# The y products of two state-space head pairs in one step, and the p·v products of two attention pairs in one step

## The chip, the cores and the metric

The kernel runs on one core of a Trainium2 chip. The metric is the device time of one execution in microseconds (us). Three executions of the kernel before took 1226.97, 1227.45 and 1230.41 us; the median is 1227.45 us.

A core has a matrix engine (TensorE, PE in the rows; its weight loads stand apart as PEld), a vector engine (VectorE, DVE), an activation engine (ScalarE, ACT), a general engine (GpSimd, POOL) and a queue that issues transfers (SyncE, SP). TensorE writes its products to banks of PSUM, from which VectorE or ScalarE take them.

## The reference, cut to what matters

Two layers on 256 tokens of width 1024. Each layer has a mixer, with sparse attention (16 heads of 64) and a state-space part (4 groups of 8 heads of 64) in parallel, and then a feed-forward part. The two products that the change touches are the last line of attention and the diagonal term of the scan:

```python
p = jax.nn.softmax(s, axis=-1).astype(v.dtype)
return jnp.einsum("bhqk,bqkhd->bqhd", p, vg)
...
cb = jnp.einsum("bclgn,bcsgn->bgcls", cm_c, bm_c)
y_diag = jnp.einsum("bgcls,bgrcls,bcsgrp->bclgrp", cb, decay, xs_c)
```

All is in float32. The sequence is a single chunk of 256 tokens, so that `y_diag` is the whole scan. In each layer this makes 8 pairs of attention heads and 16 pairs of state-space heads.

## The kernel before, in words

**The stream.** Most of TensorE's work is the big projections. A weight unit of 512 columns by 4 blocks of 128 rows lands in `st`, ScalarE rounds it into `wh`, and VectorE makes the rest `wl = st - wh` ("the split"). The activations are kept as two such parts as well (`h` for the normed input, `u` for attention's output). Each product is three matmuls in rounded float32: high by high, high by low, low by high. A unit's matmuls run feature block by feature block; after each 12 of them a function `pump` is called.

**The side work.** Attention, the scan and the norms are generators, kept in lists (`hot`, `warm`, `calm`, `cool`). Every `pump` may advance each list by one step. A step first yields a `Need`: it goes on when the tiles that it names are expected to be ready and the number of PSUM banks that it names is free. Only the first generator of `calm` advances, and `attention` and `ssd` are both in `calm`, one behind the other. A planner with its own table of costs estimates when each instruction ends; from that it decides when a step is due, and in what order VectorE, ScalarE and GpSimd get their work. So the order of the instructions is fixed when the program is built, and a change to one step can move many others. `cool` holds the stream of modulation weights (`ad`), which VectorE sums into `adacc` (eight steps, then a small product with `ones`).

**`ssd(g)`** runs for each group of four head pairs. It transposes the inputs into two tiles `xdt`, and then loops over n. A step with n below 4 makes the decay tile `e` of pair n (a product with `sel`, three activations, and a multiplication with `cbm` on VectorE). Two steps later come the y products of that pair: into one bank `py`, four matmuls, two of 256 and two of 128 columns, whose weights are 64 columns wide, so that the two heads of the pair stand in the two halves of the bank. VectorE adds the result to `x_[i]` with the weight `dsk`. When all four are done `ssd_norm(g)` starts; in it `spread` sends the reciprocal root over the partitions, and the normed results are split in two parts for the product with `w_ssm_o`. The last two of group 3 lie in the two `xdt` tiles.

**`attention`** runs twice for each layer, with four pairs. A step makes the scores of pair n, two steps later the transposes of its weights into `pT`, and one step after that its p·v products, four matmuls of the same shapes as those of y, into a bank `po`; `hi_lo` takes that bank in two parts.

In the rows, both `e` and `pT` bear the name `p`; `bk` is a PSUM bank, and `bk<-p,xdt` is a y product, `bk<-p,u` a p·v product. "128*64" is the shape of the weights: 128 rows by 64 columns. A float32 matmul that isn't rounded shows as two matmuls in the trace, so a y block of four shows as x8. All operations bear the line of the helper that records them (L209).

Of the kernel before, what the change touches and what calls it, by code (L numbers as in the profile page):

```python
# [15 lines left out]
ALU = mybir.AluOpType  # L16
# [3 lines left out]
P = 128  # L20
S = 256
# [25 lines left out]
def trunk(ctx, tc, x, c, positions, w_ada, b_ada, norm1_g, w_in, q_norm_g, k_norm_g, ssm_conv_w, ssm_conv_b,  # L47
# [1289 lines left out]
    def mixer(l, link, link_out):  # L1337
# [244 lines left out]
        def attention(heads):  # L1582
# [4 lines left out]
            for n in range(len(pairs) + TD + PD):  # L1587
                if n < len(pairs):
                    i = pairs[n]
                    yield Need(qT[i], kT[i], m01, banks=2)  # L1590
                    pss = [bank(), bank()]
                    both(pss, qT[i], kT[i], False)
                    done(qT[i], kT[i])
                    for j in range(2):
                        mm(pss[j][:, 0:384], nident, m01, False, True)
                    pe = pes[n] = hold(w_tile("pe", [P, 2, 384]))
                    mx = w_tile("mx", [P, 2, 2])
                    sums = w_tile("sums", [P, 2, 2])
                    with urgent():
                        for j in range(2):  # L1600
                            V.tensor_reduce(mx[:, j, 0:1], pss[j][:, 0:P], axis=AX.X, op=ALU.max)
                            V.tensor_reduce(mx[:, j, 1:2], pss[j][:, P:384], axis=AX.X, op=ALU.max)
                            V.tensor_tensor(mx[:, j], mx[:, j], nrq[:, 2 * i + j, :], op=ALU.mult)
                        for j in range(2):
                            for t, cs in HALF:
                                A.activation(pe[:, j, cs], pss[j][:, cs], AF.Exp, scale=rq[:, 2 * i + j, t:t + 1],
                                             bias=mx[:, j, t:t + 1], accum_out=sums[:, j, t:t + 1])
                    yield Need(sums, on="dve")
                    with urgent():
                        V.reciprocal(sums, sums)  # L1610
                        for j in range(2):
                            for t, cs in HALF:
                                G.tensor_scalar(pe[:, j, cs], pe[:, j, cs], sums[:, j, t:t + 1], 0.0, op0=ALU.mult, op1=ALU.add)
                if n - TD in pes:
                    pe = pes.pop(n - TD)
                    yield Need(pe, banks=2)
                    pT = pTs[n - TD] = hold(w_tile("pT", [P, 2, 384]))
                    pts = [bank(), bank()]
                    for j in range(2):
                        for b in range(3):  # L1620
                            T.transpose(pts[j][:, b * P:b * P + P], pe[:, j, b * P:b * P + P], ident)
                    done(pe)
                    with urgent():
                        for j in range(2):
                            A.activation(pT[:, j], pts[j][:, 0:384], AF.Copy)
                if n - TD - PD in pTs:
                    pT = pTs.pop(n - TD - PD)
                    i = pairs[n - TD - PD]
                    yield Need(pT, *vt[0][i // 4], *vt[1][i // 4], banks=1)
                    po = bank()  # L1630
                    for t, cs, src in ((0, slice(0, S), slice(0, S)), (1, slice(P, S), slice(S, 384))):
                        for j in range(2):
                            hh = 2 * i + j
                            vs = slice((hh % 4) * 64, (hh % 4) * 64 + 64)
                            mm(po[64 * j:64 * j + 64, cs], vt[t][hh // 8][(hh % 8) // 4][:, vs], pT[:, j, src], t == 0, t == 1)
                    done(pT)
                    if i % 2 == 1:
                        done(*(vt[t][i // 4][(i % 4) // 2] for t in range(2)))
                    with urgent():
                        hi_lo(po[:, 0:S], oT, i)  # L1640


        def ev_conv(base, dst, then=None):
# [44 lines left out]
        def ssd(g):  # L1688
# [12 lines left out]
            for n in range(4 + 2):  # L1701
                if n < 4:
# [13 lines left out]
                    yield Need(e, on="dve")  # L1716
                    with urgent():
                        V.tensor_tensor(e, e, cbm[g][:, None, :].to_broadcast([P, 2, 384]), op=ALU.mult)
                if n >= 2:
                    i = n - 2  # L1720
                    e = es.pop(i)
                    yield Need(e, cbm[g], *xdt, banks=1)
                    py = bank()
                    for cs, x, src in ((slice(0, S), xdt[0], slice(0, S)), (slice(P, S), xdt[1], slice(S, 384))):
                        for j in range(2):
                            hs = slice((2 * i + j) * 64, (2 * i + j) * 64 + 64)
                            mm(py[64 * j:64 * j + 64, cs], x[:, hs], e[:, j, src], x is xdt[0], x is xdt[1])
                    done(e)
                    m = 4 * g + i
                    with urgent():  # L1730
                        V.scalar_tensor_tensor(x_[i], x_[i], dsk[:, l, m:m + 1], py[:, 0:S], op0=ALU.mult, op1=ALU.add)
            while None in z_:
                yield
            warm.append(ssd_norm(g))
# [203 lines left out]
```

## Time and profile before

| | |
|---|---|
| median of three executions | 1227.45 us |
| the profiled execution, its own time | 1227.39 us |
| its span in the trace | 1225.7 us |
| TensorE busy | 1201.3 us, 98% of the span |
| VectorE busy | 991.4 us, 81% |
| ScalarE busy | 775.3 us, 63% |
| GpSimd busy | 494.1 us, 40% |

The span is the time from the first to the last instruction; 1.7 us of the execution lie outside it. "Busy" of TensorE counts a matmul from its start to its modelled end, and matmuls overlap, so the distance from one start to a later one tells more than the durations. In a window's row the fields are the stretch, its length, busy time (with the number of instructions) of TensorE, its weight loads, VectorE, ScalarE and GpSimd, then the granted TensorE clock (1.00 is 2.4 GHz, 0.50 is 1.2 GHz), the share of the DMA engines and GB/s.

### The profile page before, as it was taken

The page shows a single profiled execution, that of the slowest core. Times are in us where ns is not written, and L with a number is a line of the kernel's source. Part 1 is how long each engine was busy: PE and PEld are TensorE (multiplying, and loading weights), DVE is VectorE, ACT ScalarE, POOL GpSimd, SP SyncE. Part 2 cuts the span into 40 slices and gives each one's busy share as a digit, 9 for nine tenths or more (in the row PEclk, how much of TensorE's full clock was granted, in tenths as well). Part 3 has the DMA queues.
Part 4 walks back from the last instruction along what each step waited for, and adds up shares of the span by engine and source line. Part 5 has one row for each costly group of instructions (what it writes and reads, how often), then busy time and mean ns, then how long its engine had stood idle before and what let it go on. Part 6 is the DMA issues. An engine that isn't in the chain of part 4 may idle for free.

```text
span 1225.7 us, 24837 instructions
## 1 busy us (share of the span) xinstructions
PE 1201.3 (98%) x9835; PEld 1118.9 (91%) x9835; DVE 991.4 (81%) x1549; ACT 775.3 (63%) x1397; POOL 494.1 (40%) x503
## 2 busy tenths in 40 slices
PE   8999999999999999999999999999999999999998
PEld 7777898899988999999998778899999999999998
DVE  5488998778988789989767899888778757988863
ACT  4365577767865468778535557878578535877742
POOL 2163442216445225766202356314605313457710
PEclk9999999999999999999999999999999999999999
DMA  9765656655557666777665566264664665667551
GB/s 307 241 208 178 200 180 212 207 193 195 190 181 241 232 198 198 240 240 260 206 229 186 204 206 199 87 215 134 216 218 156 211 220 189 190 198 232 179 205 64
DMA packets 158665, 246.55 MB, mean 201 GB/s; under 512 B 11868, under 2 KB 66870, under 8 KB 158549
## 3 DMA queue, kind: packets, MB, share of 16 engines
q1 hardware_dynamic: 157989, 244.77, 60.1%
q8 instruction: 77, 1.26, 0.4%
q14 instruction: 39, 0.32, 0.1%
q0 software_dynamic: 288, 0.19, 0.1%
q10 hardware_dynamic: 272, 0.00, 0.0%
HBM read 243.89 MB, written 1.05 MB: 200 GB/s over the span
## 4 chain that ended last, share of the span: by engine, by line
PE 81%; DVE 12%; ACT 2%; issue 2%; POOL 1%; DMA 1%; SPq 0%; DVEq 0%; POOLq 0%; ACTq 0%
PE bk L209 81%; DVE wl L209 5%; DVE w L209 2%; DVE adacc L209 1%; ACT wh L209 1%; DVE p L209 1%; DVE u L209 1%; DVE t L209 1%; ACT w L209 1%; POOL rr L209 0%; DMA ad<-in_w_ada_dram 0%; POOL rows L209 0%; DVE top L209 0%; DVE mx L209 0%; POOL w L209 0%
## 5 line engine op out<-in xcount | busy, mean ns | idle before, releaser
L209 PE MATMUL bk<-h,wh 128*128 128x256 f32 x3296 | 588.1, 281 | 1.2 <-ACT h L209 1.1
L209 PEld LDWEIGHTS bk<-h,wh 128*128 128x128 f32 x3296 | 500.9, 189 | 12.0 <-issue 8.2
L209 DVE TENSOR_TENSOR wl<-st,wh 128x2048 fp32r<-128x2048 f32 (+1 forms) x200 | 439.8, 2206 | 67.3 <-ACT wh L209 67.0
L209 PE MATMUL bk<-h,wl 128*128 128x256 f32 x1648 | 457.9, 278 | 1.7 <-DVE wl L209 1.7
L209 ACT ACTIVATE wh<-st 128x2048 fp32r<-128x2048 f32 (+1 forms) x200 | 352.8, 1770 | 154.8 <-PE bk L209 129.9
L209 POOL TENSOR_TENSOR w<-w,w 128x254 f32<-128x254 f32 (+2 forms) x213 | 254.9, 1209 | 252.7 <-DVE w L209 173.4
L209 PEld LDWEIGHTS bk<-h,wl 128*128 128x128 f32 x1648 | 309.9, 188 | 2.4 <-DVE wl L209 1.9
L209 PE MATMUL bk<-u,wh 128*128 128x256 f32 x1312 | 232.6, 280 | 0.0
L209 PEld LDWEIGHTS bk<-u,wh 128*128 128x128 f32 x1312 | 199.3, 189 | 2.4 <-issue 2.4
L209 PE MATMUL bk<-u,wl 128*128 128x256 f32 x656 | 182.7, 278 | 0.6 <-DVE wl L209 0.6
L209 PE MATMUL bk<-wh,h 128*128 128x512 f32 x448 | 145.9, 402 | 3.1 <-DVE t L209 2.0
L209 ACT ACTIVATE w<-bk,vec 128x256 f32<-128x256 f32 (+2 forms) x256 | 119.7, 519 | 37.5 <-DVE w L209 26.0
L209 PEld LDWEIGHTS bk<-u,wl 128*128 128x128 f32 x656 | 123.2, 188 | 0.8 <-DVE wl L209 0.8
L209 DVE SCALAR_TENSOR_TENSOR adacc<-ad,chalf,adacc 128x512 f32<-128x512 f32 x140 | 119.0, 850 | 0.5
L209 PEld LDWEIGHTS bk<-wh,h 128*128 128x128 f32 x448 | 81.5, 188 | 23.9 <-issue 3.7
L209 POOL TENSOR_TENSOR u<-u,u 128x256 f32<-128x256 f32 (+1 forms) x56 | 74.1, 1348 | 63.1 <-DVE u L209 37.3
L209 PE MATMUL bk<-wl,h 128*128 128x512 f32 x224 | 88.7, 396 | 2.8 <-DVE wl L209 2.7
L209 DVE SCALAR_TENSOR_TENSOR w<-bk,vec,w 128x255 f32<-128x255 f32 (+1 forms) x176 | 80.3, 476 | 13.4 <-ACT w L209 11.9
L209 POOL TENSOR_TENSOR rr<-ss,mhalf 128x16 f32<-128x16 f32 x8 | 35.6, 4454 | 77.7 <-DVE ss L209 77.7
L209 POOL TENSOR_SCALAR p<-p,sums 128x128 f32<-128x128 f32 x64 | 35.6, 574 | 55.5 <-DVE sums L209 47.8
L209 ACT ACTIVATE u<-bk 128x128 f32<-128x128 f32 (+2 forms) x128 | 32.1, 321 | 39.8 <-PE bk L209 39.2
L209 PEld LDWEIGHTS bk<-wl,h 128*128 128x128 f32 x224 | 42.1, 188 | 13.4 <-DVE wl L209 4.6
(225 smaller groups left out, 1399.6 us busy)
## 6 DMA issues: line engine op xcount, KB each, us to landing
st<-in_w_in_dram SPq DMA_DIRECT2D x80, 1024.0 KB, 5.1
st<-in_w_up_dram SPq DMA_DIRECT2D x88, 512.0 KB, 5.2
ad<-in_w_ada_dram SPq DMA_DIRECT2D x160, 256.0 KB, 5.4
st<-in_w_down_dram SPq DMA_DIRECT2D x20, 1024.0 KB, 5.0
st<-in_w_ssm_o_dram SPq DMA_DIRECT2D x16, 1024.0 KB, 5.0
st<-in_w_ada_dram SPq DMA_DIRECT2D x16, 512.0 KB, 9.6
st<-in_w_attn_o_dram SPq DMA_DIRECT2D x8, 1024.0 KB, 5.1
st<-in_w_out_dram SPq DMA_DIRECT2D x8, 1024.0 KB, 5.1
```

The source lines that it names most:

```text
L209: w.issue()
```

## The change

Both loops now wait until two pairs are ready and write their products one behind the other. In `ssd` the y products of pairs 0 and 1 stand in step 3 (before: 2 and 3), those of pairs 2 and 3 in step 5 (before: 4 and 5). In `attention` the p·v products of pairs 0 and 1 stand in step 4 (before: 3 and 4), ahead of that step's transposes (before: behind them), and those of pairs 2 and 3 in step 6 (before: 5 and 6). The `Need` names both pairs' tiles, and two banks in place of one. Matmuls and their operands stay the same.

```diff
--- before.py
+++ after.py
@@ -1611,6 +1611,21 @@
                         for j in range(2):
                             for t, cs in HALF:
                                 G.tensor_scalar(pe[:, j, cs], pe[:, j, cs], sums[:, j, t:t + 1], 0.0, op0=ALU.mult, op1=ALU.add)
+                if (n - TD - PD) % 2 == 1 and n - TD - PD in pTs:
+                    two = [(pTs.pop(k), pairs[k]) for k in (n - TD - PD - 1, n - TD - PD)]
+                    yield Need(*(t for pT, i in two for t in (pT, *vt[0][i // 4], *vt[1][i // 4])), banks=2)
+                    for pT, i in two:
+                        po = bank()
+                        for t, cs, src in ((0, slice(0, S), slice(0, S)), (1, slice(P, S), slice(S, 384))):
+                            for j in range(2):
+                                hh = 2 * i + j
+                                vs = slice((hh % 4) * 64, (hh % 4) * 64 + 64)
+                                mm(po[64 * j:64 * j + 64, cs], vt[t][hh // 8][(hh % 8) // 4][:, vs], pT[:, j, src], t == 0, t == 1)
+                        done(pT)
+                        if i % 2 == 1:
+                            done(*(vt[t][i // 4][(i % 4) // 2] for t in range(2)))
+                        with urgent():
+                            hi_lo(po[:, 0:S], oT, i)
                 if n - TD in pes:
                     pe = pes.pop(n - TD)
                     yield Need(pe, banks=2)
@@ -1623,21 +1638,6 @@
                     with urgent():
                         for j in range(2):
                             A.activation(pT[:, j], pts[j][:, 0:384], AF.Copy)
-                if n - TD - PD in pTs:
-                    pT = pTs.pop(n - TD - PD)
-                    i = pairs[n - TD - PD]
-                    yield Need(pT, *vt[0][i // 4], *vt[1][i // 4], banks=1)
-                    po = bank()
-                    for t, cs, src in ((0, slice(0, S), slice(0, S)), (1, slice(P, S), slice(S, 384))):
-                        for j in range(2):
-                            hh = 2 * i + j
-                            vs = slice((hh % 4) * 64, (hh % 4) * 64 + 64)
-                            mm(po[64 * j:64 * j + 64, cs], vt[t][hh // 8][(hh % 8) // 4][:, vs], pT[:, j, src], t == 0, t == 1)
-                    done(pT)
-                    if i % 2 == 1:
-                        done(*(vt[t][i // 4][(i % 4) // 2] for t in range(2)))
-                    with urgent():
-                        hi_lo(po[:, 0:S], oT, i)
 
 
         def ev_conv(base, dst, then=None):
@@ -1716,19 +1716,19 @@
                     yield Need(e, on="dve")
                     with urgent():
                         V.tensor_tensor(e, e, cbm[g][:, None, :].to_broadcast([P, 2, 384]), op=ALU.mult)
-                if n >= 2:
-                    i = n - 2
-                    e = es.pop(i)
-                    yield Need(e, cbm[g], *xdt, banks=1)
-                    py = bank()
-                    for cs, x, src in ((slice(0, S), xdt[0], slice(0, S)), (slice(P, S), xdt[1], slice(S, 384))):
-                        for j in range(2):
-                            hs = slice((2 * i + j) * 64, (2 * i + j) * 64 + 64)
-                            mm(py[64 * j:64 * j + 64, cs], x[:, hs], e[:, j, src], x is xdt[0], x is xdt[1])
-                    done(e)
-                    m = 4 * g + i
-                    with urgent():
-                        V.scalar_tensor_tensor(x_[i], x_[i], dsk[:, l, m:m + 1], py[:, 0:S], op0=ALU.mult, op1=ALU.add)
+                if n in (3, 5):
+                    two = [(i, es.pop(i)) for i in (n - 3, n - 2)]
+                    yield Need(*(e for _, e in two), cbm[g], *xdt, banks=2)
+                    for i, e in two:
+                        py = bank()
+                        for cs, x, src in ((slice(0, S), xdt[0], slice(0, S)), (slice(P, S), xdt[1], slice(S, 384))):
+                            for j in range(2):
+                                hs = slice((2 * i + j) * 64, (2 * i + j) * 64 + 64)
+                                mm(py[64 * j:64 * j + 64, cs], x[:, hs], e[:, j, src], x is xdt[0], x is xdt[1])
+                        done(e)
+                        m = 4 * g + i
+                        with urgent():
+                            V.scalar_tensor_tensor(x_[i], x_[i], dsk[:, l, m:m + 1], py[:, 0:S], op0=ALU.mult, op1=ALU.add)
             while None in z_:
                 yield
             warm.append(ssd_norm(g))
```

In the order on TensorE, the first y products of layer 0 (group 0) stood like this before, between two matmuls of the stream; those of the next pair came 40 rows later, between two others:

```order
L209 MATMUL bk_3179<-u_2536,wh_3011 128x256
L209 MATMUL bk_3179<-u_2535,wl_3012 128x256
L209 MATMUL bk_3239<-p_495_3118,xdt_488_3062 64x256 x2
L209 MATMUL bk_3239<-p_495_3118,xdt_489_3063 64x128 x2
L209 MATMUL bk_3179<-u_2362,wh_3011 128x256
L209 MATMUL bk_3179<-u_2363,wh_3011 128x256
```

and now:

```order
L209 MATMUL bk_3175<-u_3027,wh_3096 128x256
L209 MATMUL bk_3175<-u_3026,wl_3097 128x256
L209 MATMUL bk_3276<-p_495_3116,xdt_488_3060 64x256 x2
L209 MATMUL bk_3276<-p_495_3116,xdt_489_3061 64x128 x2
L209 MATMUL bk_3277<-p_498_3155,xdt_488_3060 64x256 x2
L209 MATMUL bk_3277<-p_498_3155,xdt_489_3061 64x128 x2
L209 MATMUL bk_3175<-u_2899,wh_3096 128x256
L209 MATMUL bk_3175<-u_2900,wh_3096 128x256
```

The two blocks of four matmuls have become neighbours. The same is so at all 16 pairs of y blocks in the two layers.

The first p·v products of layer 0's attention stood alone as well, as this piece of the difference shows:

```order
 L209 MATMUL bk_2287<-h_473,wh_2103 128x256
 L209 MATMUL bk_2287<-h_472,wl_2104 128x256
-L209 MATMUL bk_2361<-p_329_2062,u_1084 64x256 x2
-L209 MATMUL bk_2361<-p_329_2062,u_1086 64x128 x2
 L209 MATMUL bk_2287<-h_297,wh_2103 128x256
 L209 MATMUL bk_2287<-h_298,wh_2103 128x256
```

They stand one step later now, with those of the second pair behind them and the transposes of `p_286` moved on:

```order
 L209 MATMUL bk_2287<-h_473,wh_2103 128x256
 L209 MATMUL bk_2287<-h_472,wl_2104 128x256
-L209 MATMUL bk_2394<-ident,p_286_1757 128x128 x3
-L209 MATMUL bk_2395<-ident,p_286_1757 128x128 x3
+L209 MATMUL bk_2376<-p_329_2062,u_1084 64x256 x2
+L209 MATMUL bk_2376<-p_329_2062,u_1086 64x128 x2
+L209 MATMUL bk_2379<-p_371_2333,u_1084 64x256 x2
+L209 MATMUL bk_2379<-p_371_2333,u_1086 64x128 x2
 L209 MATMUL bk_2286<-h_594,wh_2202 128x256
 L209 MATMUL bk_2286<-h_595,wh_2202 128x256
```

All eight pairs of p·v blocks are joined in this way. In all, 48 blocks have become 24.

On VectorE, the rows ahead of one split in layer 0 (the second unit that is split after the multiplications of group 2 have begun) were these before:

```order
L209 SCALAR_TENSOR_TENSOR w_636_4105<-bk_3925,vec_293,w_636_4105 128x255
L209 SCALAR_TENSOR_TENSOR w_636_4105<-bk_3925,vec_293,w_636_4105 128x254
L209 SCALAR_TENSOR_TENSOR adacc_3854<-ad_4001,chalf,adacc_3854 128x512
L209 TENSOR_TENSOR p_650_4197<-p_650_4197,cbm_348_2159 128x768
L209 SCALAR_TENSOR_TENSOR u_4060<-w_628_4059,w_626_4057 128x256
L209 SCALAR_TENSOR_TENSOR w_640_4109<-bk_3925,vec_293,w_640_4109 128x255
L209 SCALAR_TENSOR_TENSOR w_640_4109<-bk_3925,vec_293,w_640_4109 128x254
L209 SCALAR_TENSOR_TENSOR adacc_3854<-ad_4052,chalf,adacc_3854 128x512
L209 SCALAR_TENSOR_TENSOR u_3673<-u_3673,dsk,bk_4284 128x256
L209 SCALAR_TENSOR_TENSOR u_4108<-w_638_4107,w_636_4105 128x256
L209 SCALAR_TENSOR_TENSOR u_4112<-w_642_4111,w_640_4109 128x256
L209 TENSOR_TENSOR wl_4134<-st_3831,wh_4133 128x2048
```

and are these now:

```order
L209 SCALAR_TENSOR_TENSOR u_4067<-w_628_4066,w_626_4064 128x256
L209 SCALAR_TENSOR_TENSOR u_3699<-u_3699,dsk,bk_4209 128x256
L209 SCALAR_TENSOR_TENSOR u_4071<-w_632_4070,w_630_4068 128x256
L209 SCALAR_TENSOR_TENSOR w_640_4113<-bk_3938,vec_293,w_640_4113 128x255
L209 SCALAR_TENSOR_TENSOR u_4112<-w_638_4111,w_636_4109 128x256
L209 SCALAR_TENSOR_TENSOR w_640_4113<-bk_3938,vec_293,w_640_4113 128x254
L209 SCALAR_TENSOR_TENSOR u_3738<-u_3738,dsk,bk_4251 128x256
L209 SCALAR_TENSOR_TENSOR adacc_3995<-ad_4020,chalf,adacc_3995 128x512
L209 SCALAR_TENSOR_TENSOR u_3742<-u_3742,dsk,bk_4252 128x256
L209 SCALAR_TENSOR_TENSOR adacc_3995<-ad_4037,chalf,adacc_3995 128x512
L209 SCALAR_TENSOR_TENSOR u_4116<-w_642_4115,w_640_4113 128x256
L209 TENSOR_TENSOR wl_4138<-st_3843,wh_4137 128x2048
```

The whole stretch from the split before to this one held 22 operations, among them three multiplications `p<-p,cbm`, five `adacc` steps and two additions with `dsk`; it now holds 21, among them two, three and four. The eight convolution steps (`w<-bk,vec,w`) and the four `u<-w,w` are the same.

The order also moves the end of a layer's scan. Between the `spread` of group 3 and the first matmul that reads an `xdt` tile as a part of the scan's output stood 30 matmuls of the stream in layer 0 and 114 in layer 1; now there are 102 and 66.

## Rows read from the trace of the kernel before

**Rows 1.** Page: busy us, share of the span, instructions, by engine.

```profile
PE 1201.3 (98%) x9835; PEld 1118.9 (91%) x9835; DVE 991.4 (81%) x1549; ACT 775.3 (63%) x1397; POOL 494.1 (40%) x503
```

**Rows 2.** Windows: stretch, length, busy us by engine, TensorE clock, DMA share.

```profile
300.00:345.00 45.00, 43.27 (x371) 41.01 (x373) 42.25 (x58) 35.25 (x67) 23.39 (x21) 1.00 0.49 161
670.00:760.00 90.00, 90.00 (x498) 71.23 (x496) 84.84 (x178) 54.13 (x112) 48.49 (x36) 1.00 0.61 207
760.00:850.00 90.00, 90.00 (x770) 82.89 (x769) 76.56 (x138) 69.99 (x161) 28.37 (x39) 1.00 0.46 157
850.00:930.00 80.00, 79.84 (x699) 75.87 (x698) 62.56 (x83) 55.31 (x92) 30.87 (x28) 1.00 0.56 188
```

**Rows 3.** Groups by form: operands, shape, count, busy us, mean ns (TensorE matmuls).

```profile
L209 PE MATMUL bk<-p,xdt 128*64 128x256 f32 x128 | 21.3, 413 | 0.0
...
L209 PE MATMUL bk<-p,u 128*64 128x256 f32 x64 | 10.6, 404 | 0.0
```

**Rows 4.** Groups by form, TensorE weight loads.

```profile
L209 PEld LDWEIGHTS bk<-p,xdt 128*64 128x64 f32 x256 | 15.8, 138 | 9.2 <-issue 1.0 <-DVE wl L209 0.2
```

**Rows 5.** Timeline, 260.6 to 262.2: start, duration, engine, operation, count.

```profile
260.35 0.28 PE L209 MATMUL bk<-u,wl 128*128 128x256 f32 x1
...
260.69 0.28 PE L209 MATMUL bk<-u,wl 128*128 128x256 f32 x1
260.89 0.63 PEld L209 LDWEIGHTS bk<-p,xdt 128*64 128x64 f32 x8
260.89 0.87 PE L209 MATMUL bk<-p,xdt 128*64 128x256 f32 x8
...
261.70 0.50 PE L209 MATMUL bk<-u,wh 128*128 128x256 f32 x2
...
262.04 0.28 PE L209 MATMUL bk<-u,wl 128*128 128x256 f32 x1
```

**Rows 6.** Timeline of TensorE, 167.8 to 169.3.

```profile
167.89 0.86 PE L209 MATMUL bk<-uext,adt 128*64 128x256 f32 x4
168.68 0.51 PE L209 MATMUL bk<-h,wh 128*128 128x256 f32 x2
```

**Rows 7.** Timeline of TensorE, 766 to 769.5.

```profile
767.53 0.76 PE L209 MATMUL bk<-uext,adt 128*64 128x256 f32 x3
...
768.23 0.81 PE L209 MATMUL bk<-p,u 128*64 128x256 f32 x7
768.98 0.50 PE L209 MATMUL bk<-h,wh 128*128 128x256 f32 x2
```

**Rows 8.** Waits of TensorE: for whom, us in total, times, longest.

```profile
PE bk L209 <- DVE wl L209: 5.0, 6, 1.7
...
PE bk L209 <- ACT xdt L209: 1.2, 1, 1.2
```

**Rows 9.** Timeline of TensorE, 340.9 to 349.5, with the idle time before.

```profile
343.43 0.39 PE L209 MATMUL bk<-h,wl 128*128 128x256 f32 x1 [1.74 <-DVE wl L209]
```

**Rows 10.** Window 344 to 349, columns as in rows 2.

```profile
344.00:349.00 5.00, 5.00 (x32) 4.07 (x31) 4.47 (x7) 0.42 (x1) 4.92 (x4) 0.66 0.91 311
```

**Rows 11.** Timeline of VectorE, 318 to 344.

```profile
328.75 1.50 DVE L209 TENSOR_TENSOR p<-p,cbm 128x768 f32<-128x768 f32 x1
...
338.13 0.74 DVE L209 SCALAR_TENSOR_TENSOR adacc<-ad,chalf,adacc 128x512 f32<-128x512 f32 x1
338.90 0.48 DVE L209 SCALAR_TENSOR_TENSOR u<-u,dsk,bk 128x256 f32<-128x256 f32 x1
...
340.56 2.81 DVE L209 TENSOR_TENSOR wl<-st,wh 128x2048 fp32r<-128x2048 f32 x1
```

**Rows 12.** Timeline, 390.3 to 390.7.

```profile
390.47 0.50 PE L209 MATMUL bk<-ident,rr 128*128 128x128 f32 x3
```

**Rows 13.** Timeline of TensorE, 394.2 to 397.

```profile
394.56 0.28 PE L209 MATMUL bk<-xdt,wl 128*128 128x256 f32 x1
396.06 0.85 PE L209 MATMUL bk<-xdt,wh 128*128 128x256 f32 x2 [1.22 <-ACT xdt L209]
```

## The prediction, made before the changed kernel ran

> **What bounds the kernel now.** I read the page first: TensorE is busy for 1201.3 of 1225.7 us, VectorE for 991.4, GpSimd for 494.1 [rows 1]. So the end is set by TensorE, and a step counts by what it does to TensorE's chain of starts. An average over stages can hide a stage with another limit, so I read windows next [rows 2]. In layer 1's mixer, 670 to 930 us, TensorE has 90.00, 90.00 and 79.84 us in 90, 90 and 80, so it hardly ever waits. VectorE has 84.84 of 90 there at first, and 42.25 of 45 at the end of layer 0's scan (300 to 345): shares of 0.94, which leave little room. The list of TensorE's waits then says what it does wait for: the splits `wl`, 5.0 us in six waits, and once an `xdt` tile, 1.2 us [rows 8]. Both kinds lie near the change. The last views are timelines of TensorE around the blocks that the change joins, read by distances between starts.
>
> **The price of a block that stands alone.** Steady three-part products come in a rhythm of 0.34 us from one `wl` matmul to the next (260.35 to 260.69). With a y block between them, the distance is 1.35 us (260.69 to 262.04), so that the block costs 1.01 us [rows 5]. There are 32 such blocks (128 rows of 256 columns, four for each) and 16 of p·v (64 rows), whose matmuls last about the same, 413 and 404 ns [rows 3].
>
> **The price of one that joins another.** Once in the trace a p·v block stands behind matmuls whose weights have the same shape. In layer 0 four `uext,adt` rows stand alone: from their first start to the next full product it is 0.79 us (167.89 to 168.68) [rows 6]. In layer 1 the same four have a p·v block mixed into their end (so the row shows x3 first), and the same distance is 1.45 us (767.53 to 768.98) [rows 7]. The block that joined added 0.66 us, against 1.01 alone. The difference, 0.35 us, is what it costs to go from weights of 128 columns to weights of 64 and back, and it is paid once for a joined run. The Trainium skill (TensorEngine Tiling (Array Packing), Key Properties) says that changing the tiling mode drains TensorE, and gives no time for it; the trace agrees, with 0.35 us.
>
> **The change, part by part.** No matmul is added or removed, and no transfer; 48 blocks become 24.
>
> *Joining.* 24 joins by 0.35 us are 8.4 us less on TensorE. Nothing hides them, since TensorE is the chain that ends last. From the other side: the second block's first weights could fail to load under the first block's matmuls. A load takes 0.138 us [rows 4]; the saving would then be 0.35 - 0.14 = 0.21 us, 5.0 in all. I take 8.4, because in the joined run of rows 7 the loads are hidden, and in rows 5 all eight loads of a block (0.63 us) lie inside its matmuls' 0.87. The Trainium skill (TensorE: Matmul & The Clock Gate, Part 3: Packing small matmuls — row/col tiling) says that weight loads overlap running matmuls only where the row group differs, which these blocks' loads don't; that speaks for 5.0, and rows 5 and 7 speak against it.
>
> *The wait for `xdt`.* In layer 0, TensorE waits 1.22 us at 396.06 for the last normed part of the scan [rows 13]. That part hangs on the `spread` at 390.47 [rows 12], so the norm behind it took 5.6 us, and only 30 matmuls stood between. Now 102 stand there; at 0.34 us for three that is 11.6 us, and the wait of 1.2 us goes. In layer 1 the distance shrinks from 114 matmuls to 66, which is 7.5 us, still over 5.6: nothing is added. Bounds: 0 to 1.2.
>
> *The wait for a split.* TensorE sits idle for 1.74 us before 343.43, for the split that starts at 340.56 [rows 9, 11]. Ahead of it VectorE had a crowded stretch. After the change that stretch has one multiplication of 1.50 and two `adacc` steps of 0.74 less, and two additions of 0.48 more: 1.50 + 1.48 - 0.96 = 2.0 us less [rows 11]. TensorE itself comes there some 0.35 us earlier for a join, so about 0.1 us of the wait is left. Behind that wait the clock fell: over 344 to 349 the granted clock is 0.66 of full speed on average, which is 0.34 by 5 us = 1.7 us of lost work [rows 10]. With the wait gone I take that as gone as well. So 1.7 + 1.7 = 3.4 us less; bounds 0 (another wait takes its place) and 3.4.
>
> *New waits.* The planner has moved nearly every side step, and other splits now have the crowd ahead. No row shows what that costs. Below, it is nothing, or even a gain, if some of the other 3.3 us of waits for splits go too. Above, it is one more wait like that at 343, 3.4 us. I take 1.5, below the middle, because VectorE has no more work than before.
>
> *Two banks and held tiles.* A step that asks for two banks starts later, and holds `e` or `pT` of the first pair a step longer. Nothing on TensorE stands in line behind it: the stream's matmuls go on until the step is due. What is later is the end of the scan, and for that the distances above have room. Cost: nothing.
>
> **Sum.** 1227.39 - 8.4 - 1.2 - 3.4 + 1.5 = 1215.9 us. The profiled execution (1227.39) and the median (1227.45) are the same within 0.06, so this stands for the median as well.
>
> **The rivals.**
>
> *VectorE takes it back.* Where VectorE's share is 0.94, an earlier TensorE only waits for the next split. For it speak the shares of rows 2; against it that TensorE showed no wait at 0.94 from 670 to 760. If the wait of 3.4 us stays in some place and half of the joins are given back (4.2 us), the time is 1227.4 - 4.2 - 1.2 = 1222.0.
>
> *Weight loads stay exposed* at each join: 1227.39 - 5.0 - 1.2 - 3.4 + 1.5 = 1219.3. The joined run of rows 7 speaks against it.
>
> *Slower.* Two banks are now emptied one right behind the other by urgent work on VectorE, so a split behind them starts one more addition, 0.48 us [rows 11], later. If that showed at each of the 24 steps it would be 11.5 us, more than the 8.4 won, and with nothing else changed the time would be 1230.5. It decides from 18 of 24 on. Against it: TensorE waited for splits only six times in the whole run [rows 8], so most have room for 0.48 us.
>
> *No change.* If the 0.35 us weren't the switch but something that each block pays wherever it stands, 8.4 us would stay, and the waits that go and come would about cancel: 1227. Rows 6 and 7 speak against it.
>
> **How the numbers follow.** The forecast has 0.62; its own range is 1212.0 to 1219.5. VectorE taking it back has 0.22, exposed loads 0.06, slower 0.04, no change 0.06. The range of 1211.5 to 1222.5 holds the first case, the third and most of the second. Its lower end is the sum without new waits (1214.4), less most of the other waits for splits. About 0.3%, 3.7 us, is what a measurement of this kernel can tell from no change. Faster by more than that is below 1223.7: the first and the third case and nearly all of the second, 0.88. Within it are the no change case and the rest of the second, 0.08. Slower has 0.04.
>
> **What would show it right or wrong.** In the changed kernel's trace, a joined y block of sixteen rows between two `wl` matmuls should cost 1.66 us (1.01 + 0.66), not 2.0; at 1.8 the loads are exposed. The wait for `xdt` should be gone in layer 0. The wait before the crowded split should be under 0.5 us, and the clock 1.00 from 300 to 440. I am wrong if TensorE's waits for splits grow from 5.0 to 10 us or more, if a new drop of the clock shows in either mixer, or if a new wait at the first `w_ssm_o` products of layer 1 says that 66 matmuls weren't enough.

## The result, and the profile after

Four executions of the changed kernel took 1216.22, 1213.15, 1211.23 and 1210.65 us; the median is 1212.19, against 1227.94 for four of the kernel before. The ratio is 0.9874, with a 95% interval from 0.9845 to 0.9903. The profiled execution is the longest of the four (1216.22; span 1214.5).

The page's line of busy times and instructions, as in [rows 1]:

```profile
PE 1191.2 (98%) x9835; PEld 1115.9 (92%) x9835; DVE 992.9 (82%) x1549; ACT 775.0 (64%) x1397; POOL 481.5 (40%) x503
```

The same 9835 matmuls take TensorE 10.1 us less. VectorE has as much work as before.

TensorE's timeline of the changed kernel (start, duration, operation, count, idle time ahead), at a joined y block, at the crowded split, and at the end of each layer's scan:

```profile
265.14 0.28 PE L209 MATMUL bk<-u,wl 128*128 128x256 f32 x1
265.35 1.52 PE L209 MATMUL bk<-p,xdt 128*64 128x256 f32 x16
266.80 0.50 PE L209 MATMUL bk<-u,wh 128*128 128x256 f32 x2
267.14 0.28 PE L209 MATMUL bk<-u,wl 128*128 128x256 f32 x1
...
343.39 0.38 PE L209 MATMUL bk<-h,wl 128*128 128x256 f32 x1 [1.46 <-DVE wl L209]
...
377.86 0.71 PE L209 MATMUL bk<-ident,rr 128*128 128x128 f32 x4
...
389.88 0.28 PE L209 MATMUL bk<-u,wl 128*128 128x256 f32 x1
389.99 0.39 PE L209 MATMUL bk<-xdt,wh 128*128 128x256 f32 x2
...
964.52 0.71 PE L209 MATMUL bk<-ident,rr 128*128 128x128 f32 x4
...
972.57 0.39 PE L209 MATMUL bk<-xdt,wh 128*128 128x256 f32 x2
```

- The joined block: from `wl` to `wl` it is 267.14 - 265.14 = 2.00 us; less the 0.34 of a step without it, 1.66. Two lone blocks would be 2.02 by [rows 5], which has one at 1.01.
- The crowded split: its wait is still there, 1.46 us at 343.39, where it was 1.74 [rows 9].
- The end of the scan: the first product that reads `xdt` follows the one ahead of it by 0.11 us, without a wait. The `spread` now lies 12.1 us ahead of it in layer 0 and 8.05 us in layer 1; the wait of [rows 13] is gone.

TensorE's waits for the splits, which were 5.0 us in six waits [rows 8]:

```profile
PE bk L209 <- DVE wl L209: 5.9, 8, 1.5
```

Windows of the changed kernel (columns as in [rows 2], the TensorE clock ahead of the last two): two early stretches, the one that answers to [rows 10], and the one that the prediction named.

```profile
57.00:64.00 7.00, 5.43 (x19) 4.31 (x20) 4.91 (x7) 3.62 (x5) 0.00 (x0) 0.76 0.46 153
...
80.00:88.00 8.00, 5.98 (x21) 4.55 (x20) 6.84 (x9) 3.42 (x7) 4.92 (x3) 0.79 0.62 190
...
344.00:349.00 5.00, 5.00 (x46) 5.00 (x46) 4.72 (x7) 2.20 (x7) 3.37 (x2) 1.00 0.92 313
...
300.00:440.00 140.00, 137.14 (x1211) 132.44 (x1210) 114.20 (x158) 88.22 (x148) 52.09 (x55) 1.00 0.65 218
```

Over 344 to 349 the clock is now 1.00, and so it is over all of 300 to 440. But in this one execution it fell twice long before the first changed instruction: 0.24 x 7 + 0.21 x 8 = 3.4 us of lost work. The other three executions list a mean clock of 1.000 and are 3.1 to 5.6 us shorter.

### The profile page after: what moved, and what is told of

Read it like the earlier page. It is cut to its first block, busy times and chain, and to the rows that moved or that the text cites. A ratio compares the mean times of both kernels' runs of the same rounds, so it can differ in the third digit from the quotient of the medians.

```text
span 1214.5 us, 24832 instructions
## 1 busy us (share of the span) xinstructions
PE 1191.2 (98%) x9835; PEld 1115.9 (92%) x9835; DVE 992.9 (82%) x1549; ACT 775.0 (64%) x1397; POOL 481.5 (40%) x503
## 4 chain that ended last, share of the span: by engine, by line
PE 82%; DVE 11%; ACT 3%; issue 2%; POOL 2%; DMA 0%; SPq 0%; DVEq 0%; POOLq 0%; ACTq 0%
PE bk L209 82%; DVE wl L209 4%; DVE w L209 1%; DVE adacc L209 1%; ACT wh L209 1%; DVE u L209 1%; DVE p L209 1%; DVE t L209 1%; POOL rr L209 1%; ACT p L209 1%; ACT w L209 0%; POOL rows L209 0%; DVE top L209 0%; POOL w L209 0%; DVE sp_p L209 0%
## 5 line engine op out<-in xcount | busy, mean ns | idle before, releaser
L209 POOL TENSOR_TENSOR w<-w,w 128x254 f32<-128x254 f32 (+2 forms) x213 | 247.5, 1174 | 207.8 <-DVE w L209 169.9
L209 POOL TENSOR_TENSOR u<-u,u 128x256 f32<-128x256 f32 (+1 forms) x56 | 66.6, 1211 | 97.1 <-DVE u L209 71.3
L209 POOL TENSOR_SCALAR p<-p,sums 128x128 f32<-128x128 f32 x64 | 42.0, 674 | 52.7 <-DVE sums L209 50.0
```

What stands on the lines that cost most here:

```text
L209: w.issue()
```

## Where the time went

I compared the starts of the same stream matmuls in the two traces. Layer 0's mixer (from the stream's 780th matmul to its 2100th) went from 205.4 to 196.5 us, layer 1's mixer from 239.9 to 234.9; the two feed-forward parts changed by +0.7 and -0.7. So the gain lies where the joins lie. It splits like this:

| term | us |
|---|---|
| 24 joins; two lone blocks 2 x 0.996, one joined 1.651 (medians over the trace, less a step in the rhythm around the block): 0.34 each | -8.2 |
| wait for `xdt` in layer 0 | -1.2 |
| clock at 344 to 349 | -1.7 |
| all other waits (the split's 0.3 among them), about level | 0 |
| rhythm of the stream (below) | -2.8 |

The waits come from the distances of over 0.6 us between neighbouring starts on TensorE: they sum to 24.4 us before and 23.2 after, and the 1.2 is that for `xdt`. From 1227.4 the table makes 1213.5. The profiled execution, less its 3.4 us of early clock, is 1212.8.

**The rhythm** was not in the prediction. The stream's 256-column products run one behind the other in one of two steady rhythms, 113.4 or 117.7 ns from start to start: 0.340 or 0.353 us for three. Of the distances that I could class, 2210 were slow before (4540 fast), and 1561 after (5228 fast); I call them slow and fast intervals. 649 x 4.3 ns = 2.8 us. The last experiment shows one thing that swaps them. How long the slow rhythm then lasts hangs on what stands behind: with the same 24 joined runs the kernels below have from 1467 slow intervals (reversed order) to 2067 (one bank). So the 2.8 us is in part a draw as well, and no fixed price of the joins.

## The experiments

Two theories stood against each other. The switch theory (S): what a join saves is the change of weight shape from 128 columns to 64 and back, 0.35 us, and it saves it wherever it stands. The redraw theory (W): the planner moves side steps at any edit, so most of the gain is another draw of waits and clock. None leaves work out; three have small products more, into columns that nobody reads. Each time is set against the kernel before on the same chip (1228.56 us for the two halves, y apart and four y; 1228.21 for the two spacers, four p·v and the reversed order; 1227.24 for p·v apart, one bank and the tail).

### One half of the change at a time

The kernel before with the change's second hunk alone:

```diff
-                if n >= 2:
-                    i = n - 2
...
+                if n in (3, 5):
+                    two = [(i, es.pop(i)) for i in (n - 3, n - 2)]
+                    yield Need(*(e for _, e in two), cbm[g], *xdt, banks=2)
```

> The kernel before with the y products of two pairs in one step; attention as before. Theory S (what is won is the switch of weight shapes, 0.35 us a join): 16 joins, 5.6 us off the 1227.9 of before, so 1222.3 with waits as before; each joined y block costs 1.65 us between two products of the stream, each lone p.v block 1.00. Theory W (what is won is mostly the new order of the side work, which changes TensorE's waits): the time doesn't follow the count of joins, it may lie anywhere from 1212 to 1228, and the difference to before shows in TensorE's waits and clock, not in the blocks.

It took 1220.41 us (0.9931, 0.9911 to 0.9952): -8.2, of which 16 joins are 5.5.

The kernel before with the first hunk alone (attention):

```diff
+                if (n - TD - PD) % 2 == 1 and n - TD - PD in pTs:
+                    two = [(pTs.pop(k), pairs[k]) for k in (n - TD - PD - 1, n - TD - PD)]
...
-                if n - TD - PD in pTs:
-                    pT = pTs.pop(n - TD - PD)
```

> The kernel before with the p.v products of two pairs in one step; the scan as before. Theory S: 8 joins, 2.8 us, so 1225.1 with waits as before; each joined p.v block costs 1.65 us, each lone y block 1.00. Theory W: the time doesn't follow the count of joins.

It took 1229.14 us (1.0007, 0.9992 to 1.0022): no gain. Its joined p·v blocks are 1.654 us, as S wants, so that 2.7 us were saved and lost again. TensorE's timeline shows where that went, at the end of layer 0's scan:

```profile
390.91 0.71 PE L209 MATMUL bk<-ident,rr 128*128 128x128 f32 x4 [1.49 <-POOL rr L209]
394.16 1.25 PE L209 MATMUL bk<-u,wh 128*128 128x256 f32 x2 [2.54 <-ACT u L209]
```

and a window right behind it, that the clock fell (0.65):

```profile
394.00:401.00 7.00, 6.75 (x37) 6.29 (x38) 4.53 (x11) 1.31 (x4) 0.69 (x1) 0.65 0.77 262
```

4.0 us of waits in place of the 1.2 for `xdt`, and 0.35 x 7 = 2.5 us of clock behind them in this window, where the kernel before lost 1.7 us of clock at 344. Nothing of attention's p·v stands there; the planner put the norm's steps elsewhere. The halves alone sum to -7.6 us, the whole change gives -15.8: the parts don't add.

### The changed kernel with one half taken apart again

The second pair's y products wait for the next pump, so that the blocks stand alone, at about the changed kernel's places:

```diff
-                    yield Need(*(e for _, e in two), cbm[g], *xdt, banks=2)
+                    yield Need(*(e for _, e in two), cbm[g], *xdt, banks=1)
                     for i, e in two:
+                        if i % 2 == 1:
+                            yield Need(e, banks=1)
```

> The changed kernel, but within a step of two pairs the second pair's y products stand one pump later, 12 matmuls of the stream behind the first. Steps and held tiles as in the change, blocks apart. Theory S: 16 joins are lost, 5.6 us above the 1212.2 of the changed kernel, so 1217.8 with its waits; lone y blocks cost 1.00 each. Theory W: the order of steps is nearly that of the change, so the time stays within 2 us of 1212.2.

It took 1231.38 us (1.0024, 1.0008 to 1.0039), 19.2 above the changed kernel, where S wanted 5.6. W, put there as within 2 us of the changed kernel, missed by more: even an edit that leaves the steps nearly in place drew other waits. Two rows of its list of waits, whose longest the changed kernel doesn't have:

```profile
PE bk L209 <- DVE adt L209: 3.0, 2, 2.2
...
PE bk L209 <- ACT u L209: 1.8, 1, 1.8
```

The slow intervals rose to 2302 of 6751 (3.2 us more than in the changed kernel), and in the profiled execution the clock fell early, and once more at 393.

The same edit on the p·v products:

```diff
-                    yield Need(*(t for pT, i in two for t in (pT, *vt[0][i // 4], *vt[1][i // 4])), banks=2)
+                    yield Need(*(t for pT, i in two for t in (pT, *vt[0][i // 4], *vt[1][i // 4])), banks=1)
                     for pT, i in two:
+                        if i % 2 == 1:
+                            yield Need(pT, banks=1)
```

> The changed kernel with the y products joined and the second pair's p.v products one pump later than the first's: 8 joins fewer. S: 1212.2 + 8 x 0.35 = 1215.0 us. W: the planner draws its waits again, and the time is off that by several us, as it was with the y products apart (13.6 above what S wanted there) and with four p.v blocks in a run (5.8 above).

It took 1218.77 us (0.9916, 0.9888 to 0.9945): 3.8 over S. In it a wait for `xdt` of 1.2 us is back at the end of layer 0's scan.

### The price of the switch by itself

The changed kernel with one small product between the two blocks of each join, into columns of the bank that nobody reads. With weights of 64 columns the shape stays; with 128 it changes back and forth once more:

```diff
                         done(e)
+                        if i % 2 == 0:
+                            mm(py[0:64, 384:400], ident[:, 0:64], ones[:, 0:16], False, True)
```

(and the same behind `done(pT)`; in the second kernel `0:128` in both places for `0:64`).

> The changed kernel with a small extra matmul between the two blocks of each of the 24 joins, with weights 64 columns wide (16 columns moved, into an unused part of the first block's bank, read by nobody). Theory S: the run of one weight shape isn't broken, so a joined y block costs 1.65 us plus the extra's own 0.1 to 0.2, between 1.75 and 1.85. Rival A (what is won is only that two blocks are neighbours): as much as with the 128-column extra.

> The same extra matmul with weights 128 columns wide. Theory S: the shape changes and changes back inside the step, so the block costs 0.35 us more than with the 64-column extra, some 2.1 to 2.2 us; 24 x 0.35 = 8.4 us over that kernel's time, waits aside. Rival A: within 0.1 us of the 64-column one.

TensorE's timeline of the kernel with the narrow spacer, around one join:

```profile
265.86 0.28 PE L209 MATMUL bk<-u,wl 128*128 128x256 f32 x1
266.06 0.87 PE L209 MATMUL bk<-p,xdt 128*64 128x256 f32 x8
266.76 0.18 PE L209 MATMUL bk<-ones,ident 128*64 128x16 f32 x1
...
267.96 0.28 PE L209 MATMUL bk<-u,wl 128*128 128x256 f32 x1
```

and of the one with the wide spacer:

```profile
272.28 0.28 PE L209 MATMUL bk<-u,wl 128*128 128x256 f32 x1
272.49 0.87 PE L209 MATMUL bk<-p,xdt 128*64 128x256 f32 x8
273.29 0.40 PE L209 MATMUL bk<-ones,ident 128*128 128x16 f32 x2
273.61 0.87 PE L209 MATMUL bk<-p,xdt 128*64 128x256 f32 x8
274.41 0.50 PE L209 MATMUL bk<-u,wh 128*128 128x256 f32 x2
274.75 0.28 PE L209 MATMUL bk<-u,wl 128*128 128x256 f32 x1
```

From `wl` to `wl` it is 2.10 us with the narrow spacer and 2.47 with the wide one; less a step, 1.76 and 2.13 (medians 1.758 and 2.127). The two differ in the width of a tiny weight tile alone, and that costs 0.37 us; the rival that it is enough for two blocks to be neighbours wanted them within 0.1 us of each other. This is S's term on its own, with one reservation: the wide tile's two loads take 0.188 us each and the narrow one's 0.137, so that up to 0.10 of the 0.37 could be theirs. Whole times: 1218.27 us (0.9916, two executions) and 1223.97 (0.9963, 0.9949 to 0.9977); 5.7 apart, where 24 x 0.37 = 8.9. Part of the difference is that the second drew fewer waits: its distances of over 0.6 us sum to 21.6 us, those of the first to 23.9.

### Longer runs

All four p·v pairs of a call in one step, two to a bank, which is emptied behind its second pair:

```diff
-                if (n - TD - PD) % 2 == 1 and n - TD - PD in pTs:
-                    two = [(pTs.pop(k), pairs[k]) for k in (n - TD - PD - 1, n - TD - PD)]
+                if n - TD - PD == 3:
+                    two = [(pTs.pop(k), pairs[k]) for k in range(4)]
...
```

> The changed kernel with the p.v products of all four pairs of an attention call in its last step, two pairs to a bank and each bank emptied after its second pair. Theory S: 4 more joins, 1.4 us less than 1212.2, so 1210.8 with the changed kernel's waits; a block of four pairs costs 1.01 + 3 x 0.65 = 2.96 us. Theory W (waits redrawn by the planner outweigh the joins): anything from 1210 to 1222, with the block at 2.96 all the same.

One of its blocks and its longest new wait, in TensorE's timeline (the row ahead of the block is an `adacc` product, x8):

```profile
201.91 0.28 PE L209 MATMUL bk<-h,wl 128*128 128x256 f32 x1
202.11 0.42 PE L209 MATMUL bk<-adacc,ones 128*32 128x128 f32 x8
202.47 2.82 PE L209 MATMUL bk<-p,u 128*64 128x256 f32 x32
205.22 0.50 PE L209 MATMUL bk<-h,wh 128*128 128x256 f32 x2
...
432.70 0.28 PE L209 MATMUL bk<-h,wl 128*128 128x256 f32 x1
435.40 0.62 PE L209 MATMUL bk<-ones,w 128*128 128x16 f32 x4 [2.42 <-POOL w L209]
```

The run of 32 rows lasts 205.22 - 202.47 = 2.75 us to the next product, four times 0.69; the one such block that stands alone between matmuls of the stream costs 2.949 us, S's 2.96. The whole took 1216.62 us (0.9902, 0.9881 to 0.9923) all the same: a wait of 2.42 us for GpSimd at 435, in the feed-forward part, alone is more than the 1.4 won, and the slow intervals rose by some 300 (1.3 us).

The same with y, two pairs to a bank, but each pair taken from the bank by itself:

```diff
-                if n in (3, 5):
-                    two = [(i, es.pop(i)) for i in (n - 3, n - 2)]
+                if n == 5:
+                    two = [(i, es.pop(i)) for i in range(4)]
...
-                        py = bank()
+                        if i % 2 == 0:
+                            both_ = bank()
+                        py = both_[:, S * (i % 2):S * (i % 2) + S]
```

> The changed kernel with all four y products of a group in its last step, two pairs to a bank. Theory S: 8 more joins, 2.8 us less, so 1209.4 with the changed kernel's waits; a block of four pairs costs 1.01 + 3 x 0.65 = 2.96 us. Theory W and the rival that VectorE takes it back: four additions of 0.48 us come at once and stand ahead of splits, and TensorE's waits grow by more than 2.8 us: 1212 to 1216.

It took 1238.25 us (1.0089, 1.0061 to 1.0116). Its list of waits begins with this row:

```profile
PE bk L209 <- DVE u L209: 19.6, 16, 2.2
```

and TensorE's timeline shows the place:

```profile
268.72 0.87 PE L209 MATMUL bk<-p,xdt 128*64 128x256 f32 x8
270.54 1.52 PE L209 MATMUL bk<-p,xdt 128*64 128x256 f32 x16 [0.95 <-DVE u L209]
272.74 0.87 PE L209 MATMUL bk<-p,xdt 128*64 128x256 f32 x8 [0.68 <-DVE u L209]
```

The second pair's products wait until VectorE has added the first pair's half of the bank, twice in each of the eight groups. I had not foreseen that; S doesn't speak of it, so this run says nothing on the switch.

So I gave the changed kernel one bank for both pairs of y, emptied only behind the second:

```diff
-                    yield Need(*(e for _, e in two), cbm[g], *xdt, banks=2)
+                    yield Need(*(e for _, e in two), cbm[g], *xdt, banks=1)
...
+                        if i % 2 == 1:
+                            with urgent():
+                                for q in (i - 1, i):
+                                    V.scalar_tensor_tensor(x_[q], x_[q], dsk[:, l, 4 * g + q:4 * g + q + 1], pp[:, S * (q % 2):S * (q % 2) + S],
...
```

> The changed kernel with the y products of both pairs in the two halves of one bank, which VectorE empties only behind the second pair, so that the step asks for one bank. The switch theory (S) wants joined blocks of 1.65 us as in the changed kernel and, with other things equal, 1212.2 us. If asking for two banks held steps back and cost waits, it is faster, by 1 to 3 us. The theory that the planner's redraw decides what is left (W) wants the same blocks and a time off by several us either way.

The blocks are 1.650 us, with no wait inside. It took 1224.73 us (0.9975, 0.9956 to 0.9995), 12.5 over S: slow intervals rose to 2067, TensorE waits at the end of layer 0's scan as this row of its timeline shows, and the clock fell behind that and once near 660.

```profile
388.19 0.33 PE L209 MATMUL bk<-ident,adarow 128*128 128x128 f32 x1 [1.74 <-ACT adarow L209]
```

To ask for one bank in place of two won nothing.

### The rhythm

First I reversed the order of the matmuls inside the joined y blocks:

```diff
-                        for cs, x, src in ((slice(0, S), xdt[0], slice(0, S)), (slice(P, S), xdt[1], slice(S, 384))):
+                        for cs, x, src in ((slice(P, S), xdt[1], slice(S, 384)), (slice(0, S), xdt[0], slice(0, S))):
...
```

> The changed kernel with the two halves of a y block in reverse order, the 128-column matmuls first. Behind most y blocks the stream's matmuls run 117.7 ns apart and not 113.4 until the next side block. If the last matmuls of a block set that rhythm, the share of slow intervals moves and the time with it, by up to 2 us; if only the switch back from the 64-column shape does, the share stays and so does the time (1212, waits aside).

It took 1213.92 us (0.9884, 0.9861 to 0.9906), with blocks of 1.651 and 1467 slow intervals, against 1212.19 and 1561: the order makes no difference that these executions show. This run serves for another reading too. Its profiled execution has a mean clock of 1.000, without the early falls, and the crowded split still holds TensorE up:

```profile
340.32 0.39 PE L209 MATMUL bk<-h,wl 128*128 128x256 f32 x1 [1.45 <-DVE wl L209]
```

So that wait in the changed kernel does not come from the early falls.

Then I put a small product of 128-column weights behind each joined run:

```diff
                         done(e)
+                        if i % 2 == 1:
+                            mm(py[0:128, 384:400], ident[:, 0:128], ones[:, 0:16], False, True)
```

(and the same behind `done(pT)`).

> The changed kernel with one small matmul more behind each joined run: weights 128 columns wide, 16 moving columns, into unread columns of the second bank (24 in all). It asks what ends the slow rhythm of the stream (0.35 us from one wl product to the next, in place of 0.34), which a block of 64-column weights often leaves behind: 1561 slow intervals against 5228 fast ones in the changed kernel. If a small matmul with 128-column weights ends it, the stream behind a joined run is fast, slow intervals fall below 900, and the time is 1212.2 + 24 x 0.08 (the small matmul) - 660 x 4.3 ns = 1211.3 us or so. If the rhythm goes by something else, such as how often the width has changed, the count stays near 1560 and the time is about 1214. The switch theory (0.35 us for each change from 128 to 64 columns and back) wants the joined y block with its tail at 1.70 to 1.80 us. The planner's redraw of waits may move either by some 5 us.

It took 1218.99 us (0.991, 0.9877 to 0.9944), and slow intervals did not fall; they rose to 2238. TensorE's timeline at two joined runs, one behind the other:

```profile
264.32 0.28 PE L209 MATMUL bk<-u,wl 128*128 128x256 f32 x1
...
264.66 0.28 PE L209 MATMUL bk<-u,wl 128*128 128x256 f32 x1
264.86 1.52 PE L209 MATMUL bk<-p,xdt 128*64 128x256 f32 x16
266.31 0.40 PE L209 MATMUL bk<-ones,ident 128*128 128x16 f32 x2
...
266.88 0.28 PE L209 MATMUL bk<-u,wl 128*128 128x256 f32 x1
...
267.94 0.28 PE L209 MATMUL bk<-u,wl 128*128 128x256 f32 x1
...
268.50 1.52 PE L209 MATMUL bk<-p,xdt 128*64 128x256 f32 x16
269.95 0.40 PE L209 MATMUL bk<-ones,ident 128*128 128x16 f32 x2
...
270.51 0.28 PE L209 MATMUL bk<-u,wl 128*128 128x256 f32 x1
...
271.53 0.28 PE L209 MATMUL bk<-u,wl 128*128 128x256 f32 x1
```

Ahead of the first run a step is 0.34 us; behind it three take 267.94 - 266.88 = 1.06 (0.353 each); behind the second, three take 1.02 (0.34 each). The first run swapped the rhythm one way, the second back. So I counted, over the starts of all stream matmuls, what each y or p·v run does to the rhythm around it: before, all 37 lone blocks with readable surroundings swap it (29 from fast to slow, 8 back); in the changed kernel 21 of 22 joined ones do. With the wide spacer, which makes two trips to 64 columns in a row, 21 of 24 leave the fast rhythm as it was; with the narrow one, a single trip of as many rows, all 21 readable runs swap it. A trip to 64-column weights and back swaps the rhythm; two trips cancel. Side products with 128-column weights change it too, by no rule that I can give: before, runs of them alone end the slow rhythm in 20 of 26 cases, and bring it on in 14 of 69. The tail itself cost 0.22 us (block 1.871), more than the 0.05 to 0.15 that I had allowed.

### All times beside the price of the blocks

| kernel | time less before | blocks alone | rest |
|---|---|---|---|
| the change | -15.8 | -8.2 | -7.6 |
| reversed order | -14.3 | -8.2 | -6.1 |
| narrow spacer | -9.9 | -5.6 | -4.3 |
| wide spacer | -4.2 | +3.2 | -7.5 |
| tail | -8.3 | -2.9 | -5.4 |
| four p·v | -11.6 | -9.6 | -2.0 |
| one bank | -2.5 | -8.2 | +5.7 |
| y joined alone | -8.2 | -5.5 | -2.7 |
| p·v joined alone | +0.6 | -2.7 | +3.3 |
| p·v apart | -8.5 | -5.5 | -3.0 |
| y apart | +2.8 | -2.7 | +5.5 |

"Blocks alone" is the number of joins times the difference of the measured block medians from two lone blocks at 0.996 us (four at 3.984). S holds for the blocks of every kernel in the table; four y isn't in it, since its blocks hold waits. W, read as a draw, holds for the rest, which runs from -7.6 to +5.7. The change's rest is the best of all, level with the wide spacer's.

## Why the prediction was right, and where not

**Joins**: right, -8.2 for -8.4. The wide spacer confirms that it is the switch. The bound with exposed weight loads is out: it wanted a joined block at 1.8 us, and a block that joins adds 0.655 us (1.651 - 0.996); in the run of four, three more blocks add 0.651 each. Where the Trainium skill (TensorE: Matmul & The Clock Gate, Part 3: Packing small matmuls — row/col tiling) lets loads overlap only for differing row groups, these runs disagree. The same section also lets a load into the background weight buffer be pulled ahead; no run here shows whether that is what hides these.

**The wait for `xdt`**: right. The distances came out at 12.1 and 8.05 us, for 11.6 and 7.5.

**The crowded split**: this step failed. It put the wait at 0.1 us; it went only from 1.74 to 1.46. The part on VectorE came true, and the part on TensorE did not. VectorE's timelines begin at the split ahead and end at the start of this one. Before ([rows 11] has this split, at 340.56):

```profile
322.84 2.28 DVE L209 TENSOR_TENSOR wl<-st,wh 128x2048 fp32r<-128x2048 f32 x1
```

in the changed kernel:

```profile
325.11 2.29 DVE L209 TENSOR_TENSOR wl<-st,wh 128x2048 fp32r<-128x2048 f32 x1 [0.53 <-ACT wh L209]
...
329.35 0.96 DVE L209 TENSOR_TENSOR p<-p,cbm 128x768 f32<-128x768 f32 x1 [1.07 <-ACT p L209]
...
340.51 2.82 DVE L209 TENSOR_TENSOR wl<-st,wh 128x2048 fp32r<-128x2048 f32 x1
```

and in the reversed one:

```profile
322.05 2.29 DVE L209 TENSOR_TENSOR wl<-st,wh 128x2048 fp32r<-128x2048 f32 x1 [0.85 <-ACT wh L209]
...
337.44 2.82 DVE L209 TENSOR_TENSOR wl<-st,wh 128x2048 fp32r<-128x2048 f32 x1
```

The stretch lasts 340.56 - 322.84 = 17.7 us before and 15.4 in both others: 2.3 less, where I took 2.0, and that although VectorE now waits longer for ScalarE inside it (1.07 us at 329.35); its multiplications there last 0.96 us where they took 1.50. But I had TensorE come there only 0.35 us earlier, for one join. In the reversed kernel, which has no early falls of the clock, it is there at 340.32 - 1.45 = 338.87, before at 343.43 - 1.74 = 341.69: 2.8 us earlier, since ten joined runs stand ahead of the place (3.4 us, less some 0.65 for one y block more). The split ahead had moved up by only 0.8 us, for VectorE waited there 0.85 us for ScalarE's `wh`. So this split starts 0.8 + 2.3 = 3.1 us earlier, TensorE comes 2.8 earlier, and 0.3 us of the wait is gone. In the changed kernel's profile the early falls move both back by about 3 us, and the difference is the same. I had moved VectorE by all that it was spared, and TensorE by one join of ten.

**The clock behind that wait**: right in its size (1.7), and that was luck. I took it to go with the wait; the wait stayed and the clock held. Such falls come in some executions and not in others: the 46 other executions of the kernel before list mean clocks from 0.995 to 1.000, the four of the changed kernel 0.997 and three times 1.000, the four of the reversed one 0.997 to 1.000.

**New waits**: other splits +1.2 (5.9 - 1.46 against 5.0 - 1.74), where I took 1.5; but 0.9 of other waits went, so that 0.3 is left. None of the signs that I gave for being wrong came behind the first changed instruction: no wait at the first `w_ssm_o` products of layer 1, and the new drops of the clock, in one execution, lie ahead of all that the change moved.

**What I left out**: the rhythm, -2.8 us. Against my sum of -11.5, the terms measured make -13.9: +0.2 at the joins, +1.4 at the split, -1.2 at the new waits, -2.8 for the rhythm. The rest of the distance to 1212.2, 1.3 us, is within the spread of the four executions. So the errors went opposite ways, +1.4 at the split against -1.2 and -2.8; 1212.2 lies at the very edge of the 1212.0 to 1219.5 that I gave the forecast.

**The rivals**: VectorE took back none of the counted joins here, though its wait before the crowded split stayed. But with one bank, and with y apart, redrawn waits, clock and rhythm took back 5.5 to 5.7 us beyond the blocks. So the forecast's sign hung on the draw more than I allowed, since no rival had a price for it. Why the planner drew well for the change stays open: its waits were read, not its reasons.

## What to carry to other kernels

Between full products, a small block with narrower weights costs the change of shape as well as itself, here a third of the block's cost; so put such blocks side by side, and price the join from distances between starts, not from durations. Where a planner decides the order, every edit redraws waits of several microseconds: a gain or loss of that size beyond the counted part is no property of the edit until variants with the same counted part agree. To price a wait, move both sides of it: every saving ahead of the place brings the engine that waits there sooner. When two results share a PSUM bank, don't let the reader of the first come before the writer of the second: empty the bank once, behind both.

## What the runs showed of the hardware

- Changing from 128-column weights to 64 and back cost 0.34 to 0.37 us, by two ways of measuring it; the second can hold up to 0.10 of a longer load. The Trainium skill (TensorEngine Tiling (Array Packing), Key Properties) has the drain at a change of tiling mode; the size is from these runs.
- The stream's products have two rhythms, 113.4 and 117.7 ns, and a trip to 64-column weights swaps them (37 of 37 lone blocks, 21 of 22 joined ones). Why a trip swaps them I don't know, nor when other side products do.
- The granted clock fell in some executions and not in others, behind the same idle times: of 1.1 and 1.0 us ahead of 59 and of 2.0 us ahead of 84 in the changed kernel (0.76 and 0.79 in the two windows above), while the reversed kernel's profile has the same idle times there and a mean clock of 1.000. It fell behind the wait of 1.74 us at 343 in the kernel before, and not behind those of 1.46 and 1.45 at that place.
